# Convolution taps handed out two portions per attention round, and ten modulation chunks summed on VectorE

## The chip, the cores and the metric

The kernel runs on one core of a Trainium2 chip. The metric is the device time of one execution in microseconds (us), and the times of a kernel are told as the median of several runs. The engines are TensorE (PE in the profile, with PEld for its weight loads), VectorE (DVE), ScalarE (ACT), GpSimd (POOL) and SyncE (SP), which issues nearly all DMAs of this kernel. Each engine works through a queue of its own in order.

## What is computed

Two transformer blocks run one after the other on 512 tokens of width 1024, in float32. The first is modulated by a condition vector `c`: six rows of 1024 numbers (two shifts, two scales, two gates) come out of one product of `silu(c)` with a 1024 x 6144 matrix.

```python
def first_block(x, c, ada_w, ada_b, ...):
    c_act = jax.nn.silu(c)
    mod = c_act @ ada_w[l] + ada_b[l]
    sh1, sc1, ga1, sh2, sc2, ga2 = [m[:, None, :] for m in jnp.split(mod, 6, axis=-1)]
    h = rmsnorm(x, pre_mix_g[l]) * (1.0 + sc1) + sh1
    y = hybrid_mixer(h, ...)
    x = x + ga1 * rmsnorm(y, post_mix_g[l])
    h = rmsnorm(x, pre_ffn_g[l]) * (1.0 + sc2) + sh2
    y = swiglu_ffn(h, w_ffn_in[l], w_ffn_out[l])
    x = x + ga2 * rmsnorm(y, post_ffn_g[l])

def hybrid_mixer(h, ...):
    ...
    u = u_val * jax.nn.sigmoid(u_gate)
    u = causal_depthwise_conv(u, conv_w, conv_b)       # 512 channels, 31 taps
    u = jax.nn.silu(layernorm(u, conv_ln_g, conv_ln_b))
    y_conv = u @ w_conv_out
    o = stick_breaking_attention(q, k, v)              # 8 heads of 64
    y_att = o.reshape(b, s, ATT_WIDTH) @ w_att_out
    merged = jax.nn.sigmoid(g_conv) * y_conv + jax.nn.sigmoid(g_att) * y_att
    return merged @ w_o
```

The second block (retention heads beside latent attention heads, then a feed-forward part with a short convolution) is not touched by the change.

## The kernel before

**Products in three.** Every large product is made of three matmuls on values split into a high part and the rest (`mm3`, L204 to L207). A weight slab of 128 x 1024 is loaded by SP into one of two staging buffers `w_st`, cast by ScalarE to `w_hi` (L187), and VectorE or GpSimd forms the rest `w_lo` (L210, called from L189). During the attention rounds GpSimd does nearly all of these splits, from the merge stage on VectorE does, except for the slabs listed in `POOL_LO` (L792). Slabs are taken in the order of the list `ORDER` and loaded two ahead.

**Order.** The program's text gives the order of priority, but the planner of the tile framework (opened with `schedule_with_timeline_sim=True`, L1419) places each engine's instructions by its own estimate of when they are ready.

**Modulation in chunks.** The 1024 x 6144 matrix is taken in 24 chunks of 256 columns. A chunk is loaded as two halves `ad` of 128 x 4 x 256 (`ada_load`). `ada_acc` (L367) multiplies its eight 128 x 256 pieces by columns of `cact`, which holds `silu(c)` in the first of 32 columns and zeros beside it. The eight matmuls (L373) go four abreast, each into a strip of 32 partitions of one PSUM bank, and VectorE copies the bank to `acc` (L378). The sum over partitions is then a matmul with `ones`: `ada_cols` (L384) makes a shift column and a scale column for one block of 128 channels, and `ga_row` (L404) a quarter of a gate row, spread over all partitions. Eight chunks belong to the first norm and are done in the opening stage. Of the second norm's eight, `AD` (L773) puts six into attention rounds 3 to 8 and two (kb 6 and 7) into the merge stage. The four of the first gate are done in the merge stage (L825), the four of the second gate inside the first network's gate and up tiles (`fin_extra`, m = 4, 8, 12, 16). In the merge stage `ad` has two buffers of its own, in the network it takes both of `w_st`.

**Taps.** `conv_all` (L525) is a generator. For each j of 31 it issues one tap for each of the four channel blocks: blocks 0 to 2 are one VectorE operation each on a PSUM bank (L510, block 2 after 0 and 1 are through), block 3 is a scaled copy on ScalarE (L513) and an addition on GpSimd (L514). It pauses after every second j, so its first 15 portions are two taps of j each; then come the layer norm of the four row tiles (transposes, L540 to L546, one portion each), and from the normed rows, transposed back, `u2h` and `u2l` in two portions (L563 to L567). When the taps are through, `Banks.both` is set, and `pp()`, which hands out PSUM banks, may use the two banks of the convolution beside its own four.

**Attention rounds.** `pipeline` (L708) runs ten rounds: in round t head t's scores are made (L685 to L698, with sigmoids on ScalarE and a scan on VectorE), head t-1's weights are transposed and head t-2's output is formed. After these `stick_between(t)` adds the tiles that `STICK_FILL` lists for the round (query and key tiles of the next pair of heads, gate tiles, and in rounds 8 and 9 the convolution's output product `cout`, which reads `u2h` and `u2l`), and hands out conv portions:

```python
            step(conv, 1)
        step(conv, (30 if t == 7 else 1))
```

The first of these lines stands inside the loop over the round's tiles. Three portions are given ahead of round 0 (L591).

**Merge stage.** For four slabs p (L805) it forms the last gates, the convolution's and the attention's output product, weighs and adds them (L817, L818) and splits the sum into `mh` and `ml_`. The product with `w_o` follows.

Of the kernel before, what the change touches and what calls it, by code (L numbers as in the profile page):

```python
# [8 lines left out]
F32 = mybir.dt.float32  # L9
# [4 lines left out]
ALU = mybir.AluOpType  # L14
# [81 lines left out]
def build(tc, nc, a):  # L96
    stacks = []

    def pool(name, bufs=1, side="left", **kw):
        s = ExitStack()  # L100
        p = s.enter_context(tc.tile_pool(name=name, bufs=bufs, side=side, reuse_waits="tile", **kw))
        stacks.append(s)
        return p, s
# [13 lines left out]
    const, _ = pool("const")  # L117
    sm, _ = pool("small", 8)
    ring, _ = pool("ring")
    edge, _ = pool("edge", side="right")  # L120
    edge.tile([128, 96], F32, name="edge")
    hpool, _ = pool("hpool", side="right")

    def pt():
        ps_t = psT.tile([128, 512], F32, tag="t", name="ps_t")
        return ps_t
# [15 lines left out]
    vec = const.tile([128, NVEC], F32)  # L142
# [7 lines left out]
    zero = const.tile([128, 1], F32)  # L150
    halfpi = const.tile([128, 1], F32)
    cact = const.tile([128, 8, 32], F32)
    adab1 = const.tile([128, 48], F32)
    modA = const.tile([128, 2, 8], F32)
    modB = const.tile([128, 2, 8], F32)
    an32 = const.tile([128, 16], F32)
# [10 lines left out]
    def vcol(name, i):  # L167
        o = VOFF[name] + i
        return vec[:, o:o + 1]
# [184 lines left out]

    class ADA:
        pool, tag, bufs, nacc = ring, "st", NST, 1
        loaded = {}

    def ada_load(chunk):
        ads = []  # L360
        for hf in range(2):
            ad = ADA.pool.tile([128, 4, 256], F32, tag=ADA.tag, bufs=ADA.bufs, name="ad")
            nc.sync.dma_start(out=ad, in_=a["ada"][chunk][:, 4 * hf:4 * hf + 4, :])
            ads.append(ad)
        return ads

    def ada_acc(chunk, ap_):  # L367

        ads = ADA.loaded.pop(chunk, None) or ada_load(chunk)
        ps = pt()  # L370
        for hf, ad in enumerate(ads):
            for b in range(4):
                nc.tensor.matmul(  # L373
                    out=ps[32 * b:32 * b + 32, 0:256], lhsT=cact[:, 4 * hf + b, :], rhs=ad[:, b, :],
                    start=hf == 0, stop=hf == 1,
                )
        acc = ap_.tile([128, 256], F32, tag="acc", name="acc", bufs=ADA.nacc)
        nc.vector.tensor_copy(acc, ps[:, 0:256])  # L378
        return acc, ps[:, 256:512]

    def ada_cols(i, kb, g_name, ap_):
        acc, ps = ada_acc(8 * i + kb, ap_)
        for s in range(2):
            nc.tensor.matmul(  # L384
                out=ps[:, s:s + 1], lhsT=acc[:, s * 128:(s + 1) * 128], rhs=ones[:, 0:1], start=True, stop=True
            )
        sh, sc = 24 * i + kb, 24 * i + 8 + kb
        nc.vector.tensor_tensor(
            out=modB[:, i, kb:kb + 1], in0=ps[:, 0:1], in1=vcol("ada_b", sh), op=ALU.add
        )  # L390
        nc.vector.scalar_tensor_tensor(
            out=modA[:, i, kb:kb + 1], in0=ps[:, 1:2], scalar=adab1[:, sc:sc + 1], in1=vcol(g_name, kb),
            op0=ALU.add, op1=ALU.mult,
        )

# [41 lines left out]
    for _n in ("pre_mix_g", "pre_ffn_g"):  # L437
        _o = VOFF[_n]
        nc.vector.tensor_scalar(
            out=vec[:, _o:_o + 8], in0=vec[:, _o:_o + 8], scalar1=32.0, scalar2=None, op0=ALU.mult  # L440
        )
    _o = VOFF["ada_b"]
    nc.vector.tensor_scalar(out=adab1, in0=vec[:, _o:_o + 48], scalar1=1.0, scalar2=None, op0=ALU.add)
    nc.vector.tensor_copy(identb, ident)
    nc.vector.tensor_copy(strictb, masks[:, 0:128])
    nc.vector.tensor_copy(causalb, masks[:, 128:256])
    _o = VOFF["attn_norm_w_2"]
    nc.vector.tensor_scalar(out=an32, in0=vec[:, _o:_o + 16], scalar1=32.0, scalar2=None, op0=ALU.mult)
    _o = VOFF["mla_q_norm_w_2"]
    nc.vector.tensor_scalar(  # L450
        out=lat[:, 0:2], in0=vec[:, _o:_o + 2], scalar1=float(np.float32(16.0 * 96.0 ** -0.5)), scalar2=None,
        op0=ALU.mult,
    )
    nc.vector.tensor_scalar(
        out=lat[:, 2:3], in0=vec[:, _o + 2:_o + 3], scalar1=float(np.float32(np.sqrt(128.0))), scalar2=None,
        op0=ALU.mult,
# [123 lines left out]
    conv = conv_all()  # L580

    def step(g, n=1):
        for _ in range(n):
            next(g, None)
# [139 lines left out]
    def qk_tile(n, p):  # L724
        ps = pp()
        mtile(ps, slab(("win", WIN_OF[n] + p)), hh, hl, KB, 128)
        if n == "q":
            qk[p] = (evac_stat(ps, qkp),)
        else:
            qk[p] += evac_mov(ps, qkp)  # L730
# [3 lines left out]
    def conv_gate(m, sg):  # L734
        g = gate_tile(m)
        nc.scalar.activation(out=sg, in_=g, func=AF.Sigmoid)
        gcs[m] = sg

    def conv_out(p):
        cw = slab(("cout", p))  # L740
        for j in range(2):
            yc = pp()
            mtile(yc, cw, u2["h"], u2["l"], 4, 256, c0=128 * j)
            sg = gcs[2 * p + j]
            nc.vector.tensor_tensor(out=sg, in0=sg, in1=yc, op=ALU.mult)

    def early_gate(m):
        st = qkp.tile([128, S], F32R, tag=("st0", "st1", "ml", "mv0")[m], name="st")
        return st.bitcast(F32)

    def att_gate(m):
        g = gate_tile(m)
        nc.scalar.activation(out=gat[:, m - 8, :], in_=g, func=AF.Sigmoid)

    def stick_between(t):
        for n, m in STICK_FILL[t]:
            if n == "gate" and m >= 8:
                att_gate(m)
            elif n == "gate":
                conv_gate(m, early_gate(m))  # L760
            elif n == "cout":
                conv_out(m)
            else:
                qk_tile(n, m)
            step(conv, 1)
        step(conv, (30 if t == 7 else 1))
        for kb in range(KB):
            if AD[kb] == t:
                ada_cols(1, kb, "pre_ffn_g", accp)
        if t in (4, 6, 8):  # L770
            split_o(t // 2 - 2)
# [4 lines left out]
    def split_o(p):  # L776
        o_hi = endp.tile([128, S], F32R, name=f"oh{p}") if p < 3 else qkp.tile([128, S], F32R, tag="mv1", name="oh3")
        o_lo = endp.tile([128, S], F32R, name=f"ol{p}") if p < 2 else qkp.tile(
            [128, S], F32R, tag=("ml", "st0")[p - 2], name=f"ol{p}"
        )  # L780
        oh.append(o_hi)
        ol.append(o_lo)
        nc.scalar.copy(o_hi, ofs[p])
        lo_of(o_lo, ofs[p], o_hi, nc.gpsimd if p < 3 else nc.vector)

    qk_tile("q", 0)
    qk_tile("k", 0)
    pipeline([stick_head(h) for h in range(NH)], (2, 1, 0), stick_between)
    close(a_s, e_s, v_s)

# [9 lines left out]
    split_o(3)  # L800
    mtmp, mt_s = pool("mtmp", 4)
    grow_p, _gs = pool("growp", side="right")
    ADA.pool, ADA.tag, ADA.bufs = mtmp, "ad", 2
    grow1 = grow_p.tile([128, D], F32)
    for p in range(4):  # L805
        if p >= 2:
# [182 lines left out]
    for tt, banks in gemm_tok([("c2", i) for i in range(4)], h_operand, 416, 4, seg=2):  # L989
        b = banks[tt, 0]  # L990
# [20 lines left out]
    for kb in range(3):  # L1011
        ps = pt()
        transposes(ps, [cT[:, tt, kb * 128:(kb + 1) * 128] for tt in range(NT)])
        sc = lat[:, kb:kb + 1]
        nc.scalar.activation(out=cTh[:, kb, :], in_=ps, func=AF.Identity, scale=sc)
        nc.vector.scalar_tensor_tensor(
            out=cTl[:, kb, :], in0=ps, scalar=sc, in1=cTh[:, kb, :].bitcast(F32), op0=ALU.mult, op1=ALU.subtract
# [405 lines left out]
```

## Time and profile before

| what | us |
|---|---|
| median of 3 runs (1425.45 to 1426.05) | 1425.65 |
| the profiled execution | 1426.3 |
| its span, first to last instruction | 1424.6 |
| TensorE busy in the span | 1378.3 |
| VectorE busy | 731.9 |
| ScalarE busy | 582.1 |
| GpSimd busy | 325.1 |

The profile is of one execution. Busy time is the time in which at least one instruction of the engine was running; matmuls overlap, so a busy TensorE is not yet one at its fastest, and its pace is read from the starts of successive matmuls. The granted clock is told as a share of TensorE's full clock.

### The profile page before, as it was taken

The numbers are of one execution on the slowest core, as the hardware profiler recorded it, in microseconds if no ns is written. First come the engines' busy times: TensorE is split into PE (matmuls) and PEld (weight loads), VectorE is DVE, ScalarE is ACT, GpSimd is POOL, SyncE is SP. The second block draws the span as 40 slices with busy tenths as digits, with TensorE's granted clock in tenths as the row PEclk, the third lists the DMA queues.
The fourth block names the chain that finished last, engine by engine and source line by source line (L and its number), as shares of the span: only waits on it lengthen the run. The fifth ranks groups of instructions, "written<-read, shape, count | busy, mean of one in ns | idle before, by whom it ended". The sixth has DMA issues, their size and how long they took to land. (4 is left out here: it accounts for less than half of the span.)

```text
span 1424.6 us, 17617 instructions
## 1 busy us (share of the span) xinstructions
PE 1378.3 (97%) x6846; PEld 1119.7 (79%) x6846; DVE 731.9 (51%) x1132; ACT 582.1 (41%) x953; POOL 325.1 (23%) x329
## 2 busy tenths in 40 slices
PE   6999999999989999999999899999999999999998
PEld 4786777877878888888887788787888888888886
DVE  3299868254365332232333754688256655554334
ACT  4457655322244222222223525668345333333222
POOL 2189745321150000000002533377220000000000
PEclk9998999999999999999999999999999999999999
DMA  9422133564323344333232322001233323232321
GB/s 332 139 83 81 58 103 108 170 201 146 133 68 118 126 126 132 112 104 104 89 104 79 126 95 89 30 16 60 83 110 104 101 92 104 89 104 89 104 90 73
DMA packets 44324, 152.20 MB, mean 107 GB/s; under 512 B 4881, under 2 KB 7057, under 8 KB 44241
## 3 DMA queue, kind: packets, MB, share of 16 engines
q1 hardware_dynamic: 42720, 145.90, 31.0%
q0 software_dynamic: 1376, 4.97, 0.9%
q8 instruction: 54, 0.88, 0.3%
q14 instruction: 30, 0.24, 0.1%
q10 hardware_dynamic: 144, 0.21, 0.0%
HBM read 146.86 MB, written 4.19 MB: 106 GB/s over the span
## 5 line engine op out<-in xcount | busy, mean ns | idle before, releaser
L187 ACT CAST w_hi<-w_st 128x1024 fp32r<-128x1024 f32 (+2 forms) x217 | 225.3, 1039 | 395.6 <-PE ps_p L206 125.9
L210 DVE TENSOR_TENSOR w_lo<-w_st,w_hi 128x1024 fp32r<-128x1024 f32 (+2 forms) x179 | 222.4, 1244 | 258.5 <-ACT w_hi L187 256.6
L205 PE MATMUL ps_p<-hh,w_hi 128*128 128x512 f32 (+1 forms) x740 | 278.0, 382 | 1.9 <-ACT hh L266 1.2
L206 PE MATMUL ps_p<-hl,w_hi 128*128 128x512 f32 (+1 forms) x740 | 279.1, 378 | 0.4 <-POOL hl L210 0.4
L207 PE MATMUL ps_p<-hh,w_lo 128*128 128x512 f32 (+1 forms) x740 | 277.9, 376 | 1.4 <-DVE w_lo L210 1.4
L242 POOL TENSOR_TENSOR r<-q,mhalf 128x1 f32<-128x1 f32 x36 | 21.4, 595 | 768.4 <-DVE q L238 723.9
L205 PEld LDWEIGHTS ps_p<-hh,w_hi 128*128 128x128 f32 x740 | 139.4, 190 | 30.8 <-ACT hh L266 2.5
L207 PEld LDWEIGHTS ps_p<-hh,w_lo 128*128 128x128 f32 x740 | 140.4, 190 | 27.7 <-DVE w_lo L210 2.5
L206 PEld LDWEIGHTS ps_p<-hl,w_hi 128*128 128x128 f32 x740 | 140.6, 190 | 26.0 <-POOL hl L210 1.6
L205 PE MATMUL ps_c<-hh,w_hi 128*128 128x512 f32 (+1 forms) x354 | 130.4, 368 | 3.1 <-ACT hh L266 2.0
L206 PE MATMUL ps_c<-hl,w_hi 128*128 128x512 f32 (+1 forms) x354 | 130.0, 368 | 1.1 <-POOL hl L210 1.1
L207 PE MATMUL ps_c<-hh,w_lo 128*128 128x512 f32 (+1 forms) x354 | 128.6, 363 | 0.0
L210 POOL TENSOR_TENSOR w_lo<-w_st,w_hi 128x1024 fp32r<-128x1024 f32 (+1 forms) x38 | 93.1, 2455 | 67.0 <-ACT w_hi L187 47.1
L210 DVE TENSOR_TENSOR gl<-gf,gh 128x512 fp32r<-128x512 f32 x44 | 30.4, 690 | 105.6 <-ACT gh L869 105.5
L869 ACT CAST gh<-gf 128x512 fp32r<-128x512 f32 x44 | 27.4, 622 | 135.1 <-PE ps_p L206 124.1
L205 PEld LDWEIGHTS ps_c<-hh,w_hi 128*128 128x128 f32 x354 | 67.3, 190 | 15.9 <-ACT hh L266 2.5
L206 PEld LDWEIGHTS ps_c<-hl,w_hi 128*128 128x128 f32 x354 | 66.9, 189 | 11.7 <-POOL hl L210 1.3
L207 PEld LDWEIGHTS ps_c<-hh,w_lo 128*128 128x128 f32 x354 | 67.1, 189 | 11.0 <-issue 0.8
L207 PE MATMUL ps_p<-w_hi,gl 128*128 128x512 f32 x176 | 68.5, 389 | 0.0
L206 PE MATMUL ps_p<-w_lo,gh 128*128 128x512 f32 x176 | 68.5, 389 | 0.0
L205 PE MATMUL ps_p<-w_hi,gh 128*128 128x512 f32 x176 | 68.5, 389 | 0.0
L510 DVE SCALAR_TENSOR_TENSOR ps_c<-upad,vec,ps_c 128x512 f32<-128x512 f32 x87 | 60.6, 747 | 0.7
(423 smaller groups left out, 2536.0 us busy)
## 6 DMA issues: line engine op xcount, KB each, us to landing
ad<-in_ada SPq DMA_DIRECT2D x48, 512.0 KB, 4.0
w_st<-in_w_fin SPq DMA_DIRECT2D x44, 512.0 KB, 3.7
w_st<-in_w_up SPq DMA_DIRECT2D x44, 512.0 KB, 3.7
w_st<-in_w_win SPq DMA_DIRECT2D x22, 512.0 KB, 3.7
w_st<-in_w_fout SPq DMA_DIRECT2D x22, 512.0 KB, 3.6
w_st<-in_w_down SPq DMA_DIRECT2D x22, 512.0 KB, 3.7
w_st<-in_w_gate SPq DMA_DIRECT2D x16, 512.0 KB, 3.7
w_st<-in_w_wo SPq DMA_DIRECT2D x16, 512.0 KB, 3.7
```

The costliest lines, as they stand in the source:

```text
L187: nc.scalar.copy(w_hi[:, :n], w_st[:, :n])
L205: nc.tensor.matmul(out=out, lhsT=lh, rhs=rh, start=start, stop=False)
L206: nc.tensor.matmul(out=out, lhsT=lh, rhs=rl, start=False, stop=False)
L207: nc.tensor.matmul(out=out, lhsT=ll, rhs=rh, start=False, stop=stop)
L210: (eng or nc.vector).tensor_tensor(out=out, in0=src, in1=hi.bitcast(F32), op=ALU.subtract)
L242: nc.gpsimd.tensor_tensor(out=r, in0=q, in1=mhalf[:, 0:1], op=ALU.pow)
L510: nc.vector.scalar_tensor_tensor(out=out, in0=src, scalar=w, in1=acc, op0=ALU.mult, op1=ALU.add)
L869: nc.scalar.copy(gh, gf[:, k, :])
```

## The change

Four things are edited.

1. In `stick_between` the portion after each tile goes away, and the round's last line gives two portions in place of one (30 in round 7, as before). Rounds 0 to 6 gave 3, 2, 3, 2, 3, 3 and 3 portions and now give two each.
2. `ADA` gets a flag `vector`. It is set where the merge stage switches `ADA` to its own buffers, and not reset. With it `ada_acc` makes `acc` on VectorE, with one product and seven products with addition of 128 x 256, each by the column of `cact` that holds `silu(c)`, and issues no matmul and no copy. A PSUM bank is still taken for the matmul with `ones`.
3. The constant `1 + ada_b` is no longer kept as a tile of its own (`adab1`, 48 columns): the two groups of eight columns that are used are raised by one in place in `vec`.
4. The spacer `edge` shrinks from 96 to 16 columns.

```diff
-    edge.tile([128, 96], F32, name="edge")
+    edge.tile([128, 16], F32, name="edge")
...
-    adab1 = const.tile([128, 48], F32)
...
-        loaded = {}
+        loaded, vector = {}, False
...
         ads = ADA.loaded.pop(chunk, None) or ada_load(chunk)
+        if ADA.vector:
+            acc = ap_.tile([128, 256], F32, tag="acc", name="acc", bufs=ADA.nacc)
+            for hf, ad in enumerate(ads):
+                for b in range(4):
+                    cc = cact[:, 4 * hf + b, 0:1]
+                    if hf == 0 and b == 0:
+                        nc.vector.tensor_scalar(out=acc, in0=ad[:, b, :], scalar1=cc, scalar2=None, op0=ALU.mult)
+                    else:
+                        nc.vector.scalar_tensor_tensor(
+                            out=acc, in0=ad[:, b, :], scalar=cc, in1=acc, op0=ALU.mult, op1=ALU.add
+                        )
+            return acc, pt()[:, 256:512]
         ps = pt()
...
-            out=modA[:, i, kb:kb + 1], in0=ps[:, 1:2], scalar=adab1[:, sc:sc + 1], in1=vcol(g_name, kb),
+            out=modA[:, i, kb:kb + 1], in0=ps[:, 1:2], scalar=vcol("ada_b", sc), in1=vcol(g_name, kb),
...
-    nc.vector.tensor_scalar(out=adab1, in0=vec[:, _o:_o + 48], scalar1=1.0, scalar2=None, op0=ALU.add)
+    for _i in (_o + 8, _o + 32):
+        nc.vector.tensor_scalar(
+            out=vec[:, _i:_i + 8], in0=vec[:, _i:_i + 8], scalar1=1.0, scalar2=None, op0=ALU.add
+        )
...
-            step(conv, 1)
-        step(conv, (30 if t == 7 else 1))
+        step(conv, (30 if t == 7 else 2))
...
-    ADA.pool, ADA.tag, ADA.bufs = mtmp, "ad", 2
+    ADA.pool, ADA.tag, ADA.bufs, ADA.vector = mtmp, "ad", 2, True
```

## Rows read from the trace of the kernel before

**Rows 1.** The page's part 1: busy time, share of the span and instructions.

```profile
PE 1378.3 (97%) x6846; PEld 1119.7 (79%) x6846; DVE 731.9 (51%) x1132; ACT 582.1 (41%) x953; POOL 325.1 (23%) x329
```

**Rows 2.** Windows: each engine's busy us (instructions), granted clock, DMA share, GB/s.

```profile
145.00:275.00 130.00, 128.97 (x713) 100.43 (x712) 84.78 (x124) 67.95 (x129) 68.50 (x48) 1.00 0.31 101
275.00:345.00 70.00, 70.00 (x366) 51.12 (x366) 32.11 (x46) 18.38 (x24) 15.82 (x9) 1.00 0.58 197
...
440.00:600.00 160.00, 160.00 (x749) 129.63 (x748) 56.30 (x81) 41.74 (x51) 0.00 (x0) 1.00 0.39 126
```

**Rows 3.** Timeline of PE: start, us, line, operation; in brackets its wait and releaser.

```profile
115.24 0.85 PE L685 MATMUL ps_p<-mv,st 128*128 128x128 f32 x3 [2.10 <-ACT mv L616]
...
136.07 0.80 PE L685 MATMUL ps_p<-mv,st 128*128 128x512 f32 x1 [1.40 <-ACT sp L691]
...
223.54 0.55 PE L231 MATMUL ps_t<-cst,sp 128*128 128x128 f32 x3 [1.03 <-DVE of L674]
```

**Rows 4.** Windows of five us behind the second of these waits.

```profile
135.00:140.00 5.00, 3.93 (x11) 2.67 (x12) 4.97 (x10) 4.85 (x13) 4.38 (x4) 0.60 0.39 107
140.00:145.00 5.00, 5.00 (x18) 3.96 (x17) 4.97 (x6) 2.77 (x5) 4.04 (x5) 0.71 0.01 2
```

**Rows 5.** Timeline of PE around the second gate's second chunk.

```profile
501.74 0.39 PE L206 MATMUL ps_c<-hl,w_hi 128*128 128x512 f32 x1
501.97 0.39 PE L207 MATMUL ps_c<-hh,w_lo 128*128 128x512 f32 x1
502.29 1.07 PE L373 MATMUL ps_t<-ad,cact 128*32 128x256 f32 x16
...
503.63 0.40 PE L206 MATMUL ps_p<-hl,w_hi 128*128 128x512 f32 x1
```

**Rows 6.** Timeline of PE around a chunk of the merge stage.

```profile
300.69 0.40 PE L207 MATMUL ps_p<-oh,w_lo 128*128 128x512 f32 x1
301.02 0.64 PE L373 MATMUL ps_t<-ad,cact 128*32 128x256 f32 x8
...
302.27 0.64 PE L373 MATMUL ps_t<-ad,cact 128*32 128x256 f32 x8
302.84 0.50 PE L207 MATMUL ps_c<-hh,w_lo 128*128 128x512 f32 x1
303.18 0.39 PE L205 MATMUL ps_c<-hh,w_hi 128*128 128x512 f32 x1
```

**Rows 7.** Line L406: duration ns min/median/max, first and last start us, form.

```profile
L406 DVE SCALAR_TENSOR_TENSOR grow<-grow,gr x8: 414/424/426, 310.5 to 601.3; 128x256 f32<-128x256 f32 x8
```

**Rows 8.** Timeline of DVE at the start of the kernel.

```profile
5.41 0.18 DVE L443 TENSOR_SCALAR adab<-vec 128x48 f32<-128x48 f32 x1
```

**Rows 9.** Line L510: the last taps of blocks 0, 1 and 2.

```profile
L510 DVE SCALAR_TENSOR_TENSOR cacc<-upad,vec,ps_c x3: 734/734/748, 117.1 to 158.9; 128x512 f32<-128x512 f32 x3
```

**Rows 10.** The convolution's end: statistics (L540), u2l (L210), first product reading u2h.

```profile
L540 DVE BATCH_NORM_STATS2 st<-ps_p x3: 687/699/702, 191.6 to 210.7; 128x6 f32<-128x512 f32 x3
...
L210 POOL TENSOR_TENSOR u2l<-u,u2h x4: 1268/1296/1978, 226.6 to 246.5; 128x512 fp32r<-128x512 f32 x4
...
263.12 0.40 PE L205 MATMUL ps_p<-u2h,w_hi 128*128 128x512 f32 x1
```

**Rows 11.** Timeline of ACT ahead of the wait at 136 us.

```profile
134.58 0.72 ACT L513 ACTIVATE tap<-upad,vec 128x512 f32<-128x512 f32 x1
```

**Rows 12.** Timelines of POOL and DVE: two weight splits at the same time.

```profile
284.40 2.40 POOL L210 TENSOR_TENSOR w_lo<-w_st,w_hi 128x1024 fp32r<-128x1024 f32 x1 [3.39 <-ACT w_hi L187]
...
285.74 2.15 DVE L210 TENSOR_TENSOR w_lo<-w_st,w_hi 128x1024 fp32r<-128x1024 f32 x1 [7.48 <-ACT w_hi L187]
```

**Rows 13.** Timeline of DVE: a weight split of the merge stage.

```profile
296.82 1.21 DVE L210 TENSOR_TENSOR w_lo<-w_st,w_hi 128x1024 fp32r<-128x1024 f32 x1
```

**Rows 14.** Tile ad, 270 to 345 us: its loads.

```profile
DMA to landing us min/median/max: 3.6/5.5/8.9
```

## The prediction

> **What bounds the kernel now.** I read the page's engine line first: TensorE is busy 1378.3 of 1424.6 us, twice as long as the next engine [rows 1]. That is a mean, so I went to the windows by stage. In the merge stage (275 to 345 us) and the first network's gate and up tiles (440 to 600 us) PE fills every microsecond at full granted clock, while VectorE is at 32.11 of 70 and 56.30 of 160 [rows 2]. There one microsecond taken from TensorE's queue is one off the end, as long as weights and evacuations keep up. The attention rounds (115 to 275 us) are not so clean: the timeline of PE shows three waits, of 2.10, 1.40 and 1.03 us [rows 3], and behind the second the granted clock is 0.60 and then 0.71 for five microseconds each [rows 4], so it ran in part at the lower of its two levels, 1.2 GHz. From 145 on PE is busy 128.97 of 130 us [rows 2].
>
> **Chunks on VectorE.** `ADA.vector` is set ahead of the merge loop and never cleared, so all ten chunks still open there move: kb 6 and 7 and the four quarters of the first gate in the merge stage, the four quarters of the second gate in `fin_extra`. Each drops eight matmuls at L373 and the copy at L378; the matmul against `ones` (L384, L404) stays, as do the loads.
> Second gate: from the matmul at 501.97 to the one at 503.63 are 1.66 us, with one unshown matmul (L205) between; the step without a chunk is 501.97 - 501.74 = 0.23 us. The chunk costs 1.66 - 2 x 0.23 = 1.20 us [rows 5]. Four of them: 4.8 us.
> Merge: one of six lies whole (at 293.85 us), five come in two halves with other matmuls between, as their loads land. From 300.69 to 303.18 are 2.49 us and four ordinary steps (L205 and L206 stand unshown between the halves), so 2.49 - 4 x 0.23 = 1.57 us, more than the whole one because each change of shape is paid twice [rows 6]. 1.20 + 5 x 1.57 = 9.05 us. Together 13.85 us of TensorE time, all in stretches where PE never waits.
> What is added: per chunk one `tensor_scalar` and seven `scalar_tensor_tensor`, 128x256. The row of that operation and shape is L406 at 424 ns [rows 7]; the first one I cost the same, which can only be high or low by a part of one operation. 8 x 0.424 = 3.4 us a chunk, ending in `acc`. In the second gate VectorE has over 100 us free [rows 2], and the four chunks stand four pairs of tiles apart: covered. In the merge six chunks add 20.4 us to 32.11, 52.5 of the 70 - 9.05 = 61 us that are left, 86% full. That is covered too, but thinly; if the cover fails it is w_lo (L210) and the bank-freeing products at L817 that queue behind, and TensorE waits for them (rivals C and D).
> The staging buffers of `ad` are now freed by VectorE instead of by TensorE's place in its queue. For the loads behind them on SP's queue this can be earlier or later; between a gain and a loss of one landing I take nothing, since PE shows no wait on weights there.
>
> **Small edits.** One 48-column add at the start becomes two 8-column ones, in a stretch where VectorE waits for loads: the old one took 0.18 us at 5.41 [rows 8], so within 0.2 us either way, taken as nothing. `edge` and `adab1` only move addresses.
>
> **Taps.** The hand-out falls from 19 portions before round 7 (rounds of three or two) to 14 (two each), beside the three given at the start. One would expect VectorE, ScalarE and GpSimd to be relieved in rounds 0 and 1. The trace speaks against it. The last tap of block 0 was written at 117.1 us [rows 9], when head 0's scores had only begun (115.24) [rows 3]. This is tap 61 of blocks 0 and 1, so portion 11 (six of them to a portion), the last that round 2 hands out: the planner runs taps as filler, two rounds ahead of their place in the program, wherever its own estimate has a free slot. A portion handed out one round later still again stands behind everything of rounds 0 and 1, as it already does. So I expect taps to run at nearly the same times, ending near 160 us as now, and the waits at 115 and 136 us to stay. I value this at nothing, with a bound of -4.3 us (rival A) on the good side.
> What does move is what TensorE itself does at the conv's end: the eight groups of four transposes around the layer norm. TensorE is full, so they run at their place. Statistics of the four row tiles now start at 191.6 and the last at 210.7, and the last `u2l` starts at 246.5 [rows 10]; the first two tiles go to the end of round 6, everything else to the end of round 7. The wait of 1.03 us at 223.5, on VectorE, stood amid this work and may go; I leave it out. `Banks.both` turns true at the end of round 6 instead of round 4, so for two more rounds scores and gates share four PSUM banks. Rounds 2 and 3 already ran so, without a PE wait [rows 2, 3]: nothing, bounded by the 1.40 us of the one wait that showed with four banks.
>
> **The sum.** Against the profiled execution of 1426.3 us (span 1424.6): 1426.3 - 13.85 = 1412.5. The median of the runs is 1425.65, 0.65 lower, so 1411.8.
>
> **Rivals.**
> A. Taps lose against stick work after all. Just ahead of the wait at 136.07 ScalarE ran a tap of 0.72 us [rows 11] while the sigmoids that free the score bank stood behind it. If its later hand-out displaces it and the wait drops far enough that the clock holds, 1.40 us go and, by the clocks of 0.60 and 0.71, 2.0 + 1.45 us less the half of 1.07 us that PE was idle in there: 2.9. Total 4.3, so 1407.5. Against it: the whole argument on filler above.
> B. The conv's end comes too late. `u2h` is first read at 263.1 [rows 10], 15 us after `u2l` is done. Now all of it hangs behind round 7's gate tiles. About 14 us of chain (my estimate from [rows 10]: some eleven steps of 0.8 us from a row tile's transposes over statistics, `upad`, sigmoid and cast to the first `u2h`, then four splits of 1.3 us) stand against two gate tiles of 24 x 0.23 = 5.5 us each, one chunk of 1.2 and the heads' transposes and products, some 15 to 18 us. If three weight splits on GpSimd of 2.4 us [rows 12] come between, it is some 3 us late, and a clock drop like the one above makes it 6: 1418. For it: the same chain now takes from 210.7 to 246.5. Against it: VectorE was full with scans there and the steps were spread over two rounds.
> C. VectorE becomes the merge stage's bound. While GpSimd ran a split from 284.40 to 286.8, VectorE's split of the same kind took 2.15 us [rows 12], against 1.21 alone [rows 13]. GpSimd is busy 15.82 us in this stage [rows 2]; if three quarters of it lengthened VectorE's work, 52.5 becomes 64 of 61 us: 3 us over, and one clock drop of 2.9: 1418.
> The Trainium skill, "SBUF — State Buffer", section "Who interferes with whom", speaks against the change here: a VectorE instruction with two SBUF inputs and a GpSimd instruction that reads SBUF exclude each other for the whole instruction. The seven adding operations of a chunk have two SBUF inputs, so by that rule rival C is what happens wherever GpSimd works; the split of 2.15 us agrees with it. The sum stays with the free 424 ns, because GpSimd is idle for most of the stage.
> D. Slower. Place: VectorE's queue in the merge. A chunk's operation that waits for its `ad` half holds everything behind it, the weight splits above all. Halves there land in 3.6 to 8.9 us, median 5.5 [rows 14]; a split done at 298.0 is first needed at 302.84 [rows 6, 13], a slack of 4.8. Where the queue is held for longer, TensorE stands and falls to 1.2 GHz: 1.0 + 2.9 = 3.9 us a time. Twelve halves would cost 47 us; the gain turns into a loss from 14 to 17 us on, four or five of them. With six, one per chunk, 23 us: 1435. Against it: PE takes the same loads in order today, in a queue that is just as strict, and its windows there are full [rows 2].
>
> **How the numbers follow.** Forecast 1411.8: 0.62. A (1407.5) 0.12, B (1418) 0.12, C (1418) 0.08, D (1435) 0.04; 0.02 for shifts in later stages' order. The range takes in the forecast, A, B and C with about 2.5 us around them: 1405 to 1420.5. A measurement of this kernel can tell about 0.2%, 2.9 us, from no change. Faster by more than that: forecast, A, most of B and C, 0.89; within 0.06, a part of B and C that comes out together; slower 0.05.
>
> **What would show it.** Right: no L373 matmuls after 275 us and 80 new VectorE operations of about 0.42 us; the stage from 275 to 345 shorter by about 9 us and the next by 4.8, PE still without waits in both; the waits at 115 and 136 us and their lower clock as before; block 0's last tap still near 117 us; layer-norm statistics in two groups, some 30 us later than now. Wrong: a PE wait on `u2l` (B), on `acc`, `w_lo` or L817's banks (C, D), or tap times that moved by a round (A).

## The result, and the profile after

The changed kernel takes 1413.95 us (median of four runs, 1412.32 to 1415.18) against 1425.61 us before: 0.9917 of the time, 95% interval 0.9900 to 0.9934, so 11.7 us less. The forecast was 1411.8 us. The direction and the size of the main term hold, but the gain is made up otherwise than forecast: a loss behind `w_o` and a gain in the latent heads were not in the sum, and they cancel in part.

The profiled execution took 1415.18 us, the longest of the four; its span is 1413.5. The page's part 1 of the changed kernel, to be read beside [rows 1]:

```profile
PE 1365.6 (97%) x6686; PEld 1118.4 (79%) x6686; DVE 765.0 (54%) x1203; ACT 582.5 (41%) x953; POOL 325.5 (23%) x329
```

TensorE has 12.7 us less busy time and 160 matmul records fewer (two for each of the ten chunks' 80 matmuls, as x16 for eight in [rows 5] and x8 for four in [rows 6]); VectorE has 33.1 us more. The windows, with the columns of [rows 2]:

```profile
275.00:345.00 70.00, 68.80 (x308) 56.78 (x308) 52.51 (x83) 21.27 (x27) 14.99 (x9) 1.00 0.62 198
440.00:600.00 160.00, 160.00 (x707) 132.44 (x706) 70.89 (x112) 42.83 (x53) 0.00 (x0) 1.00 0.43 133
```

VectorE did take up the work: 52.51 us in place of 32.11 in the first window, and TensorE, which had none before, now has one wait there, of 1.20 us, on a chunk's `acc`. In the second window TensorE stays full.

To see where the time went, this table cuts each profiled execution at starts of matmuls: the start up to the first product with `oh` (A), from there to the last one with `oh` (B, the merge stage), to the last one with `mh` or `ml_` (C, the product with `w_o`), to the first one with `gh` (D, the norm behind `w_o` and the first network's gate and up tiles), to the first one with `kT` (E), and to the last one with `kT` (F, the latent heads). From there to the start of the last matmul are 421.1 to 421.4 us in every kernel. The other rows are experiments, told below. The stages of a row are of one profiled execution, which lies up to 2.4 us from the median beside it (merge_only).

| kernel | A | B | C | D | E | F | median |
|---|---|---|---|---|---|---|---|
| before | 288.3 | 66.9 | 43.8 | 260.8 | 277.7 | 58.7 | 1425.61 |
| after | 290.2 | 58.0 | 44.2 | 259.0 | 277.5 | 56.3 | 1413.95 |
| small_only | 288.4 | 66.8 | 43.8 | 260.8 | 276.6 | 58.8 | 1425.94 |
| taps_only | 288.6 | 66.9 | 43.8 | 260.8 | 276.6 | 58.7 | 1426.27 |
| taps_one | 290.0 | 56.6 | 44.2 | 259.0 | 276.6 | 58.8 | 1416.58 |
| gate2_only | 288.4 | 67.0 | 43.8 | 255.7 | 277.7 | 56.3 | 1418.14 |
| merge_only | 288.1 | 56.6 | 44.2 | 264.2 | 276.6 | 58.7 | 1420.59 |
| vector_only | 288.6 | 57.8 | 44.2 | 259.2 | 276.6 | 56.4 | 1412.59 |
| few_products | 288.2 | 57.5 | 43.8 | 255.7 | 276.5 | 56.3 | 1408.81 |
| twice | 288.6 | 55.7 | 58.8 | 261.9 | 276.6 | 56.5 | 1429.00 |
| last_bank | 287.8 | 70.7 | 41.7 | 255.4 | 277.8 | 58.8 | 1423.57 |
| last_on_pe | 288.9 | 58.0 | 45.0 | 255.5 | 276.5 | 58.7 | 1412.86 |
| two_acc | 288.0 | 60.9 | 43.8 | 255.7 | 276.6 | 56.3 | 1411.38 |
| two_acc_old | 288.4 | 60.7 | 43.8 | 255.7 | 275.5 | 56.3 | 1411.55 |

From before to after: A +1.9, B -8.9, C +0.4, D -1.8, E -0.2, F -2.4; with the rest -11.1, which is 1426.3 less 1415.18. B is near the forecast of 9.05. D should have been -4.8. F was not expected to move at all.

**What is late in D.** The timeline of PE behind the product with `w_o`, first of the kernel before, then of the changed one:

```profile
399.69 0.44 PE L231 MATMUL ps_t<-cst,xn 128*128 128x128 f32 x2 [0.35 <-DVE xn L255]
401.58 0.39 PE L205 MATMUL ps_c<-hh,w_hi 128*128 128x256 f32 x1 [1.45 <-ACT hh L266]
```

```profile
396.18 0.44 PE L230 MATMUL ps_t<-cst,xn 128*128 128x128 f32 x2 [3.31 <-DVE xn L254]
399.80 0.58 PE L204 MATMUL ps_c<-hh,w_hi 128*128 128x256 f32 x1 [3.18 <-ACT hh L265]
```

Two waits of 1.80 us together became 6.49. Both are on the chain of the norm: the normed rows `xn` of the second row tile (row tile 1), then `hh` made from the transposes. Row tile 1 goes through ScalarE, VectorE and GpSimd behind row tile 0, so the chain starts when row tile 0 of the product is complete, and that tile lies in the two banks `ps_t` (psT has two). These lines of PE show when the last quarter of the first gate is multiplied with `ones`, in one of those two banks; first the kernel before, then the changed one:

```profile
342.01 0.59 PE L404 MATMUL ps_t<-acc,ones 128*128 128x256 f32 x2
...
355.41 0.39 PE L205 MATMUL ps_t<-w_hi,mh 128*128 128x512 f32 x1
```

```profile
348.45 0.39 PE L204 MATMUL ps_c<-w_hi,mh 128*128 128x512 f32 x1
...
359.81 0.59 PE L418 MATMUL ps_t<-acc,ones 128*128 128x256 f32 x2
360.05 0.58 PE L204 MATMUL ps_t<-w_hi,mh 128*128 128x512 f32 x1
```

Before, that quarter was done 13.4 us ahead of the first product with `mh`, and row tile 0 began first. After, its product stands 11.4 us behind the first product with `mh`, and row tile 0 begins only behind it. The last matmul of tile 0 then stood 12.2 us ahead of the end of the product, where it stood 14.3 us ahead of it before. VectorE's own lines tell why the quarter is late: its sum could not begin before TensorE had read the quarter before it (at 347.09), since there is one buffer `acc`, and the sum of 3.7 us of work took until 356 among splits and products. The product with `ones` then ran 3.8 us later, at the place that the planner gave it; TensorE shows no wait in front of it.

```profile
348.06 0.34 DVE L378 TENSOR_SCALAR acc<-ad,cact 128x256 f32<-128x256 f32 x1
349.26 0.48 DVE L380 SCALAR_TENSOR_TENSOR acc<-ad,cact,acc 128x256 f32<-128x256 f32 x1
351.39 2.04 DVE L380 SCALAR_TENSOR_TENSOR acc<-ad,cact,acc 128x256 f32<-128x256 f32 x2
353.95 2.04 DVE L380 SCALAR_TENSOR_TENSOR acc<-ad,cact,acc 128x256 f32<-128x256 f32 x4
```

A second thing stands in the way of the chain. On ScalarE the two weight casts of the first network came behind the sum of squares of row tile 1 before, and come ahead of it now. First the kernel before, then the changed one:

```profile
396.88 1.06 ACT L250 ACTIVATE junk<-x 128x1024 bf16<-128x1024 f32 x1 [4.15 <-POOL x L337]
397.94 1.04 ACT L187 CAST w_hi<-w_st 128x1024 fp32r<-128x1024 f32 x1
```

```profile
390.62 2.00 ACT L186 CAST w_hi<-w_st 128x1024 fp32r<-128x1024 f32 x2 [2.33 <-PE ps_p L206]
392.54 1.05 ACT L249 ACTIVATE junk<-x 128x1024 bf16<-128x1024 f32 x1
```

Behind them the order differs in two more places. On VectorE two weight splits, which need these casts, now run ahead of `q`, the step between that sum of squares and `xn`; on ScalarE one more cast, which waits for its slab, now stands ahead of `hh`. The kernel before, then the changed one:

```profile
398.06 0.16 DVE L236 TENSOR_TENSOR q<-ss,eps1k 128x1 f32<-128x1 f32 x1 [2.36 <-ACT junk L250]
400.97 1.01 ACT L266 ACTIVATE hh<-ps_t,modB,modA 128x256 fp32r<-128x256 f32 x2
```

```profile
391.71 2.92 DVE L209 TENSOR_TENSOR w_lo<-w_st,w_hi 128x1024 fp32r<-128x1024 f32 x2 [0.44 <-ACT w_hi L186]
394.56 0.14 DVE L235 TENSOR_TENSOR q<-ss,eps1k 128x1 f32<-128x1 f32 x1
398.24 1.05 ACT L186 CAST w_hi<-w_st 128x1024 fp32r<-128x1024 f32 x1 [3.12 <-DMA w_st<-in_w_fin]
399.19 1.01 ACT L265 ACTIVATE hh<-ps_t,modB,modA 128x256 fp32r<-128x256 f32 x2
```

Counted from the start of row tile 0's last matmul (384.65 us before, 380.23 after), row tile 1's sum of squares starts 12.2 us behind it in the kernel before and 12.3 in the changed one, so the two casts hold it up by no more than 0.1 us. `q` starts 13.4 us behind it and now 14.3: the splits cost 0.9. From the transposes to `hh` it was 1.28 us and is 3.01, with the cast in between. Of the 4.7 us that the two waits grew, the late row tile by itself thus accounts for some 2.1 (14.3 less 12.2), the order on VectorE and ScalarE for some 2.6. Whether this order follows from the late quarter, or comes without it, is what the experiments had to tell.

### The profile page after: what moved, and what is told of

Read it like the earlier page. It is cut to its first block, busy times and chain, and to the rows that moved or that the text cites. A ratio compares the mean times of both kernels' runs of the same rounds, so it can differ in the third digit from the quotient of the medians.

```text
span 1413.5 us, 17378 instructions
## 1 busy us (share of the span) xinstructions
PE 1365.6 (97%) x6686; PEld 1118.4 (79%) x6686; DVE 765.0 (54%) x1203; ACT 582.5 (41%) x953; POOL 325.5 (23%) x329
## 4 chain that ended last, share of the span: by engine, by line
PE 86%; DVE 5%; DMA 3%; ACT 2%; issue 2%; POOL 2%; SPq 0%; POOLq 0%; ACTq 0%; DVEq 0%
PE ps_p L204 17%; PE ps_p L206 17%; PE ps_p L205 17%; PE ps_c L204 7%; PE ps_c L205 7%; PE ps_c L206 7%; PE ps_t L230 2%; PE ps_t L204 2%; PE ps_t L206 2%; PE ps_t L205 2%; DVE w_lo L209 1%; PE ps_t L667 1%; PE ps_t L387 1%; DMA ad<-in_ada 1%; ACT w_hi L186 1%
## 5 line engine op out<-in xcount | busy, mean ns | idle before, releaser
L206 PE MATMUL ps_p<-hh,w_lo 128*128 128x512 f32 (+1 forms) x756 | 285.0, 378 | 1.4 <-DVE w_lo L209 1.4
L205 PE MATMUL ps_p<-hl,w_hi 128*128 128x512 f32 (+1 forms) x756 | 286.0, 379 | 0.4 <-POOL hl L209 0.4
L204 PE MATMUL ps_p<-hh,w_hi 128*128 128x512 f32 (+1 forms) x756 | 283.4, 383 | 1.9 <-ACT hh L265 1.2
L206 PEld LDWEIGHTS ps_p<-hh,w_lo 128*128 128x128 f32 x756 | 144.1, 191 | 28.4 <-DVE w_lo L209 2.5
L204 PEld LDWEIGHTS ps_p<-hh,w_hi 128*128 128x128 f32 x756 | 142.4, 191 | 30.0 <-ACT hh L265 2.5
L205 PEld LDWEIGHTS ps_p<-hl,w_hi 128*128 128x128 f32 x756 | 144.2, 191 | 26.6 <-POOL hl L209 1.6
L204 PE MATMUL ps_c<-hh,w_hi 128*128 128x512 f32 (+1 forms) x338 | 123.7, 366 | 4.0 <-ACT hh L265 3.2
L205 PE MATMUL ps_c<-hl,w_hi 128*128 128x512 f32 (+1 forms) x338 | 124.6, 369 | 0.4 <-POOL hl L209 0.4
L206 PE MATMUL ps_c<-hh,w_lo 128*128 128x512 f32 (+1 forms) x338 | 122.4, 362 | 0.0
L205 PEld LDWEIGHTS ps_c<-hl,w_hi 128*128 128x128 f32 x338 | 64.2, 190 | 10.3 <-POOL hl L209 0.6
```

The lines of the kernel that those rows point to most:

```text
L204: nc.tensor.matmul(out=out, lhsT=lh, rhs=rh, start=start, stop=False)
L205: nc.tensor.matmul(out=out, lhsT=lh, rhs=rl, start=False, stop=False)
L206: nc.tensor.matmul(out=out, lhsT=ll, rhs=rh, start=False, stop=stop)
```

## The experiments

**Theory.** The gain is TensorE's time for the ten chunks; the taps are worth nothing; D loses some 3 us to the late last quarter. **Rivals**: the taps bring a part; VectorE bounds the merge stage; the casts by themselves make D late.

### One part at a time

taps_only is the kernel before with this edit:

```diff
-            step(conv, 1)
-        step(conv, (30 if t == 7 else 1))
+        step(conv, (30 if t == 7 else 2))
```

> The kernel before with the tap hand-out of the change alone (two portions at each round's end). Theory: the planner runs taps as filler wherever its own estimate has a free slot, so they keep their times (block 0's last tap near 118 us, block 2's near 159 us), the waits of 2.1 us at 115 us and 1.4 us at 136 us stay, and only the layer norm's statistics move, to about 230 to 248 us. Time 1424 to 1428 us, that is 0 to +2 us against the kernel before. Rival: a part of the gain of 11.7 us is the taps'; then the wait at 136 us goes or the clock behind it holds, and the time is 1422 us or less.

1426.27 us, ratio 1.0008 (0.9999 to 1.0017): nothing, as expected. The last taps of blocks 0 to 2, where [rows 9] has 117.1 to 158.9, and the waits of [rows 3]:

```profile
L510 DVE SCALAR_TENSOR_TENSOR cacc<-upad,vec,ps_c x3: 732/734/747, 117.7 to 159.5; 128x512 f32<-128x512 f32 x3
...
115.78 0.67 PE L685 MATMUL ps_p<-mv,st 128*128 128x128 f32 x3 [2.10 <-ACT mv L616]
136.97 0.50 PE L685 MATMUL ps_p<-mv,st 128*128 128x512 f32 x1 [1.40 <-ACT sp L691]
```

The taps kept their times although their hand-out moved, and both waits stay. The wait of 1.03 us at 223.5 is gone in this kernel, but A is no shorter (288.6 for 288.3).

small_only has the spacer and the constant alone:

```diff
-    edge.tile([128, 96], F32, name="edge")
+    edge.tile([128, 16], F32, name="edge")
...
-    nc.vector.tensor_scalar(out=adab1, in0=vec[:, _o:_o + 48], scalar1=1.0, scalar2=None, op0=ALU.add)
+    for _i in (_o + 8, _o + 32):
...
```

> The kernel before with only the spacer's size and the constant 1 + ada_b changed. Theory: within 1 us of the kernel before, with its waits in the latent heads (1.15, 1.43 and 1.28 us) and behind the product with w_o as there: 1424.5 to 1426.5 us. Rival: the moved addresses or the other order bring the 2.5 us that the latent heads gain wherever the second gate's chunks run on VectorE: 1423 us.

1425.94 us, ratio 1.0003 (0.9994 to 1.0011): nothing.

vector_only is the changed kernel with the old hand-out, the reverse of the first diff.

> The changed kernel with the old tap hand-out, so the ten chunks on VectorE and the small edits alone. Theory: the whole gain is TensorE's time for the chunks, 8.9 us in the merge stage and 4.8 us in the second gate, less about 3 us behind the product with w_o, and a shift of up to 2.5 us in the latent heads that is the planner's: 1411 to 1415 us. Rival (the taps bring a part): 1417 us or more.

1412.59 us, ratio 0.9904 (0.9891 to 0.9918). The ten chunks carry the whole gain. merge_only and gate2_only, with the old hand-out too, divide it: merge_only sets the flag back behind the merge stage, gate2_only sets it only there.

```diff
-    ADA.pool, ADA.tag, ADA.bufs = ring, "st", NST
+    ADA.pool, ADA.tag, ADA.bufs, ADA.vector = ring, "st", NST, False
```

> The kernel with the old tap hand-out and only the six merge-stage chunks on VectorE (the flag is set back ahead of the product with w_o). Theory: -8.9 us in the merge stage and about +3 us behind the product with w_o, where the norm chain starts late: 1418 to 1421 us, with the stage from the first to the last oh product near 58 us in place of 66.9. Rival: nothing is lost behind w_o by these chunks, the loss comes from elsewhere: 1416.5 to 1417.5 us.

> The kernel with the old tap hand-out and only the four second-gate chunks on VectorE (the flag is set behind the merge stage). Theory: 4 x 1.20 us off TensorE, nothing else: 1420 to 1421.5 us, and the waits behind the product with w_o as in the kernel before (about 1.8 us). Rival: the VectorE work of these chunks holds up evacuations and eats a part: 1422 us or more.

merge_only took 1420.59 us (its five runs from 1418.15 to 1422.34), 0.9963 (0.9951 to 0.9976). In the table, which shows its fastest execution, B is 10.3 us shorter and D 3.4 us longer, so the loss in D belongs to these six chunks. Its timeline of PE shows the three signs at once:

```profile
356.30 0.59 PE L418 MATMUL ps_t<-acc,ones 128*128 128x256 f32 x2
...
392.67 0.44 PE L230 MATMUL ps_t<-cst,xn 128*128 128x128 f32 x2 [3.32 <-DVE xn L254]
396.33 0.58 PE L204 MATMUL ps_c<-hh,w_hi 128*128 128x256 f32 x1 [3.22 <-ACT hh L265]
```

gate2_only took 1418.14 us, 0.9946 (0.9933 to 0.9960): more gain than the 4.8 us expected. D gives 5.1 us, that is 1.27 a chunk, with the waits behind `w_o` as before; the other 2.4 us are in F, 300 us behind the edit. TensorE waits there for `sp`, the exponentials that ScalarE makes; the kernel before first, then gate2_only:

```profile
947.83 0.50 PE L205 MATMUL ps_c<-cTh,w_hi 128*128 128x512 f32 x1 [1.15 <-ACT sp L1201]
968.96 0.50 PE L205 MATMUL ps_p<-cTh,w_hi 128*128 128x512 f32 x1 [1.43 <-ACT sp L1201]
977.83 0.50 PE L205 MATMUL ps_p<-cTh,w_hi 128*128 128x512 f32 x1 [1.28 <-ACT sp L1201]
```

```profile
942.81 0.50 PE L204 MATMUL ps_c<-cTh,w_hi 128*128 128x512 f32 x1 [0.27 <-ACT sp L1218]
970.37 0.50 PE L204 MATMUL ps_p<-cTh,w_hi 128*128 128x512 f32 x1 [0.43 <-ACT sp L1218]
```

In F ScalarE, VectorE and GpSimd run the same instructions in another order (most of the group norm's steps `va` and `rs` stand one to three microseconds sooner). Over the fourteen kernels F has just two levels, 58.7 to 58.8 and 56.3 to 56.5, seven kernels at each. All seven at the lower level have the second gate's chunks on VectorE, but these chunks do not decide it alone: last_bank, last_on_pe and taps_one have them too and stand at the upper level. What goes with the level is the planner's order; why it falls one way or the other stays open.

### What VectorE's work costs

few_products keeps two of a chunk's eight products, twice adds a second operation behind each:

```diff
-                    else:
+                    elif b == 0:
                         nc.vector.scalar_tensor_tensor(
```

> The changed kernel with two of a chunk's eight VectorE products (the first of each half; the other six are left out, so the modulation rows are not the right ones). Tells what the VectorE work of the change costs beside TensorE. Theory: it costs TensorE nothing but the last quarter's lateness, so 1409 to 1412 us, most of it as smaller waits behind the product with w_o. Rival (VectorE bounds the merge stage in part): the merge stage gets shorter by more than 2 us too, 1408 us or less.

1408.81 us, 5.1 us below the changed kernel and 0.2 below the range expected. The merge stage hardly moves (B 57.5 for 58.0, with 0.2 us of waits on `acc` left of 1.20), so VectorE held it up by about that one wait and did not bound it. Another 3.7 us are in C and D, where the waits are those of the kernel before again:

```profile
390.22 0.44 PE L230 MATMUL ps_t<-cst,xn 128*128 128x128 f32 x2 [0.35 <-DVE xn L254]
392.11 0.39 PE L204 MATMUL ps_c<-hh,w_hi 128*128 128x256 f32 x1 [1.45 <-ACT hh L265]
```

Between the two profiled executions another 2.0 us lie in A, ahead of the chunks, and 1.0 in E.

```diff
+                    nc.vector.scalar_tensor_tensor(
+                        out=acc, in0=ad[:, b, :], scalar=zero, in1=acc, op0=ALU.mult, op1=ALU.add
+                    )
```

> The changed kernel with a second operation of the same form behind each of a chunk's eight (it adds zero times the piece), so VectorE does about 3.9 us more for each chunk. Theory: the merge stage has 58 us and VectorE 52.5 us of work there already; 23 us more do not fit, TensorE waits on acc, w_lo or banks for some 10 to 20 us there, while the four chunks of the second gate stay covered: 1424 to 1436 us. Rival (the cover is wide, since VectorE's rows next to GpSimd only look long): under 1418 us.

1429.00 us, 15.1 above the changed kernel: the size expected, in another place. B is not longer (55.7); the chunks slide behind it, and TensorE stands in C, which grows by 14.6 us. Its waits, and its window from 365 to 375 us:

```profile
363.61 0.70 PE L421 MATMUL ps_t<-acc,ones 128*128 128x256 f32 x2 [2.18 <-DVE acc L383]
373.11 1.22 PE L421 MATMUL ps_t<-acc,ones 128*128 128x256 f32 x2 [8.80 <-DVE acc L383]
...
365.00:375.00 10.00, 1.89 (x5) 1.52 (x6) 8.15 (x19) 0.00 (x0) 0.00 (x0) 0.50 0.78 278
```

TensorE is busy 1.89 of 10 us, and its granted clock is 0.50, the lower level. So the cover of the merge stage is real but ends below twice this work, and what gives way first are the last quarters, not the weight splits.

### The late quarter

last_bank takes the last quarter's product out of psT:

```diff
+            if chunk == 19:
+                ps_l = psP.tile([128, 512], F32, tag="p", name="ps_l")
+                return acc, ps_l[:, 256:512]
             return acc, pt()[:, 256:512]
```

> The changed kernel with one thing else: the last of the first gate's four quarters forms its product with ones in a bank of psP, not in one of the two of psT that row tile 0 of the product with w_o needs next. Theory: the late quarter (its product ran at 359.81 us, 11.4 us behind the first product with mh) no longer holds tile 0, its matmuls start with the others, the norm chain runs about 2 us sooner against TensorE's end of the product, and the waits of 3.31 and 3.18 us behind it fall to about 0.4 and 1.5 as in the kernel before: 1409 to 1411.5 us. Rival: the weight casts ahead of the norm chain on ScalarE are the cause by themselves, and the waits stay above 5 us in sum: 1413 to 1415 us.

The time, 1423.57 us, is a miss for both; the waits answer the question.

```profile
336.31 0.70 PE L421 MATMUL ps_t<-acc,ones 128*128 128x256 f32 x2 [3.94 <-DVE acc L380]
342.89 0.70 PE L421 MATMUL ps_l<-acc,ones 128*128 128x256 f32 x2 [3.32 <-DVE acc L380]
...
400.93 0.44 PE L230 MATMUL ps_t<-cst,xn 128*128 128x128 f32 x2 [0.35 <-DVE xn L254]
402.82 0.38 PE L204 MATMUL ps_c<-hh,w_hi 128*128 128x256 f32 x1 [1.45 <-ACT hh L265]
```

The waits behind `w_o` are 0.35 and 1.45, as before the change, and D is 255.4. The price was paid earlier: the planner now put the quarters' products ahead of the last gate tile, and TensorE waited for `acc` three times, 8.0 us in all, in a merge stage that grew to 70.7. Some 2 us of that are products with `mh` that moved into it from C (41.7), and between 335 and 350 us the granted clock was 0.69 to 0.84. So this run changes the order as well as the bank.

last_on_pe leaves that one chunk to TensorE:

```diff
-        if ADA.vector:
+        if ADA.vector and chunk != 19:
```

> The changed kernel with one chunk, the last quarter of the first gate, back on TensorE. Theory: it costs 1.2 to 1.6 us of TensorE's time, and gives back most of what the late quarter lost: the norm chain starts about 2 us sooner against the end of the product with w_o, and the waits there fall by some 4 us: 1410 to 1412.5 us. Rival: the waits stay, and the time is 1415 us or more.

1412.86 us, just above the range expected. D falls to 255.5 (waits of 0.35 and 1.45 us), C takes 0.8 us more for the chunk's matmuls. 2.4 of the gain go back in F, which fell to the upper level.

two_acc gives `acc` a second buffer in the merge stage, in turn:

```diff
-            acc = ap_.tile([128, 256], F32, tag="acc", name="acc", bufs=ADA.nacc)
+            acc = (ADA.pool if ADA.tag == "ad" and chunk % 2 else ap_).tile([128, 256], F32, tag="acc", name="acc", bufs=ADA.nacc)
```

> The changed kernel with acc alternating between two buffers in the merge stage, so a chunk's VectorE operations no longer wait until TensorE has read the chunk before it. Theory: the sums come sooner, the last gate quarter's product with ones runs ahead of the first product with mh, row tile 0 of the product with w_o starts with the others, and the waits behind it fall from 3.3 and 3.2 us to about 0.4 and 1.5: 1408.5 to 1411 us. Rival: VectorE itself is too full in the stage, so the quarter stays late and TensorE waits for acc in its place: 1413 us or more.

> The same with the old tap hand-out, so the changed kernel's chunks on VectorE with the two acc buffers, without the tap part. Theory: the taps are worth nothing, with at most 1.5 us against them as the runs so far stand: 1407.5 to 1410.5 us and 0 to 1.5 us below the run with the new hand-out. Rival: the tap part brings something once the rest is clean, and this one is slower by over 1 us.

1411.38 us with the new hand-out of the taps, 1411.55 with the old one (0.9902 of the kernel before, 0.9889 to 0.9916, and 0.9909, 0.9895 to 0.9922): 0.4 and 1.0 us above the ranges expected, and no difference between the two hand-outs. The timeline of PE of two_acc:

```profile
309.72 0.67 PE L418 MATMUL ps_t<-acc,ones 128*128 128x256 f32 x2 [0.66 <-DVE acc L380]
316.05 0.61 PE L398 MATMUL ps_t<-ones,acc 128*128 128x1 f32 x4 [1.08 <-DVE acc L380]
342.24 0.70 PE L418 MATMUL ps_t<-acc,ones 128*128 128x256 f32 x2 [1.40 <-DVE acc L380]
...
393.44 0.44 PE L230 MATMUL ps_t<-cst,xn 128*128 128x128 f32 x2 [0.35 <-DVE xn L254]
395.33 0.39 PE L204 MATMUL ps_c<-hh,w_hi 128*128 128x256 f32 x1 [1.45 <-ACT hh L265]
```

The quarter is in time (342.24 against a first product with `mh` at 349.17), and D loses nothing: 255.7, as with the second gate's chunks alone. But three waits on `acc`, 3.1 us, now stand in B, which is 2.9 us longer. Most of the loss moved instead of going. Kernel against kernel with the same hand-out, two_acc is 2.6 us below the changed kernel, but 2.2 of that lie in A, ahead of the chunks; two_acc_old is 1.0 below vector_only, less than the runs of one kernel differ (1410.25 to 1413.59 here). Of the two readings of D, all of these runs speak for the quarter: wherever row tile 0 was done 14.3 us ahead of the product's end, as in the kernel before (last_bank, last_on_pe, two_acc, two_acc_old, few_products), the casts stood behind the norm again, the waits were 0.35 and 1.45 and D was 255.4 to 255.7; wherever it was 12.2 us (the changed kernel, vector_only, merge_only, taps_one), D was 3.3 to 3.5 us longer. The place of the casts went with the tile's in every kernel. So the order comes with the late tile, and no run has a late tile with the casts behind; by the timelines of D above, some 2.1 us of waiting would then stay, which is an estimate.

### How far ahead taps run

taps_one hands out one portion a round in place of two (`else 1` for `else 2` in the first diff).

> The changed kernel with one conv portion at the end of each round in place of two (30 in round 7, as before), so the last ten taps of each block and the whole layer norm are handed out in round 7. Theory: taps fill free slots wherever the hand-out stands, so block 0's last tap stays near 118 us and block 2's within 10 us of 160, and the statistics of the layer norm all fall behind round 7: 1412 to 1417 us. Rival: the planner reaches two rounds ahead at most; then the last taps run behind 190 us, u2l comes late and TensorE waits for it: 1420 us or more.

```profile
L527 DVE SCALAR_TENSOR_TENSOR cacc<-upad,vec,ps_c x3: 730/734/748, 117.6 to 159.4; 128x512 f32<-128x512 f32 x3
...
L557 DVE BATCH_NORM_STATS2 st<-ps_p x3: 680/681/689, 245.1 to 246.9; 128x6 f32<-128x512 f32 x3
```

The last tap again starts at 159.4 us, though a third of them is now handed out in round 7 at the earliest, and only the layer norm moves. Block 0's last tap ran at 117.6 us, and its portion, the eleventh, is now handed out in round 7. So the planner is not held to two rounds ahead. 1416.58 us, with F at its upper level.

## Why the prediction was right, and where it was wrong

**Second gate.** Forecast 1.20 us a chunk [rows 5], measured 1.27 (5.1 us in D for four).

**Merge stage.** Forecast 9.05 us, B gives 8.9. Where TensorE waits nowhere in it (merge_only, taps_one) it gives 10.3, of which about 0.4 is the last quarter's product with `ones` that moved behind it (C is 0.4 longer): some 9.9 for the six chunks, so the price was some 0.8 too low. The changed kernel pays back 1.20 in the wait on `acc`. That B comes out next to the forecast is these two errors against each other, so in part luck.

**What is added.** The operation was costed by [rows 7] at 0.424 us and takes 0.484; the reason is in the last section. That VectorE shows the forecast 52.5 us in the window is luck: the window holds five of the six chunks, which take 23.8 us there, where 20.4 were forecast for six.

**Cover: the step that failed.** The prediction added up VectorE's work, found 52.5 of 61 us, and called it covered; a failing cover was to show at `w_lo` or at the banks of L817. The total was right and the question was wrong. A chunk is a chain: load, eight operations in order, a product that reads `acc`, and only then the next chunk. With a single `acc` six chunks in a row are late together, and the last one holds one of two PSUM banks that the next stage opens with. That cost 3.3 us in D and 1.20 in B, and none of the rivals named it; the 0.4 in C is the product with `ones` that B lost. In D the two waits grew by 4.7 us, while later waits of the stage got shorter. The sum treated `pt()` as unchanged because the call still stands there, though what stands behind the bank's release had changed from a matmul to 3.7 us of VectorE work.

**Taps.** Valued at nothing, with the filler argument. taps_only shows it, taps_one and the pairs with either hand-out (the changed kernel and vector_only, two_acc and two_acc_old) agree. It was even stated too narrowly: "two rounds ahead" is no limit. The layer norm moved as forecast, to two groups from 230.3 to 248.3 us in place of [rows 10].

**The rounds.** The waits of [rows 3] at 115 and 136 us stayed at 2.10 and 1.39 us, but the clock behind the second did not: from 135 to 145 us it was 0.75 and 0.91, where [rows 4] has 0.60 and 0.71. A third wait, of 0.34 us at 149.51, came in with a granted clock of 0.66 from 150 to 155 us, which by estimate costs 5 x 0.34 = 1.7 us, as much as the higher clock from 135 to 145 us gave back. In the other thirteen profiles the clock there is 1.00, also in those with a wait of 0.16 to 0.23 us at the same place (gate2_only, merge_only, few_products, two_acc). In them A goes from 287.8 to 290.0 us without following the edits; of the 1.9 us that it lost here no part is shown to come from the change.

**Latent heads.** Not in the sum: -2.4 us. It hides most of the loss behind `w_o`. Without both, the sum would have been -8.9 - 5.1 = -14.0, near the forecast of 13.85, with the luck in B that is told above.

**Rivals.** A fell with the taps' times. B fell: the last `u2l` came 28 us later (they ran from 260.4 to 274.9 us), and TensorE never waited for it. C did not decide (few_products: B shrank by 0.5 us, where C had 3 us and a clock drop), though its mechanism is there (last section). D has the right place, a queue of VectorE that makes something late, but not the thing: it was to be `w_lo`.

## What to carry to other kernels

When work moves from a full engine to one that has time, count the chain and its buffers beside the total: how many operations must run in order before anyone may read, how many buffers let the next chain begin, and which bank the last one holds when the next stage opens. Here the planner, which orders by its own estimate, made the hand-out edit worth nothing and let a stage far away jump between two levels; take the parts apart by stage before giving an edit credit for a time.

## What the runs showed of the hardware

**A column as scalar costs VectorE 60 ns.** Two lines of the changed kernel with the same operation, shape and memory (duration ns min/median/max); the first takes its scalar from a column of `cact`, the scalar of the second is the constant 32.0:

```profile
L380 DVE SCALAR_TENSOR_TENSOR acc<-ad,cact,acc x70: 472/484/2497, 282.2 to 583.5; 128x256 f32<-128x256 f32 x70
...
L420 DVE SCALAR_TENSOR_TENSOR grow<-grow,gr x8: 414/422/425, 313.5 to 590.5; 128x256 f32<-128x256 f32 x8
```

The median is 484 against 422 ns; the row chosen for the price [rows 7] had the constant.

**VectorE next to GpSimd.** The first chunk's operations met a split on GpSimd that ran from 279.57 to 284.38 us:

```profile
279.57 4.81 POOL L209 TENSOR_TENSOR w_lo<-w_st,w_hi 128x1024 fp32r<-128x1024 f32 x2 [3.34 <-ACT w_hi L186]
...
282.17 3.54 DVE L380 SCALAR_TENSOR_TENSOR acc<-ad,cact,acc 128x256 f32<-128x256 f32 x3
...
286.35 0.48 DVE L380 SCALAR_TENSOR_TENSOR acc<-ad,cact,acc 128x256 f32<-128x256 f32 x1
```

Three of them took 3.54 us, where 1.45 is their time alone. The first took 2497 ns, from 282.17 to 284.67; GpSimd's second split ended at 284.38, and the two operations behind took 485 ns each. The Trainium skill, "SBUF — State Buffer", section "Who interferes with whom", has a VectorE instruction with two SBUF inputs and a GpSimd instruction that reads SBUF exclude each other for the whole instruction; the trace agrees with the 2497 ns of that operation. GpSimd is busy for only 14.99 us of the window, and with three quarters of these operations left out (few_products) the merge stage is only 0.5 us shorter.
